# Two-layer diffusion trunk: the order of gathered rows and of latent attention's parts, and the engine that forms the table blocks' lower parts

## The chip, the cores and the metric

The kernel runs on one core of one Trainium2 chip. The metric is the device time of one execution in microseconds (us), the median of several. One execution of the kernel was also profiled; all rows below come from that one.

## The reference, cut to what matters

512 latent tokens (four tiles of 128) and 256 context tokens (two tiles), 1024 wide, go through two layers. Layer 0 mixes with neighbourhood attention and a gated delta net, layer 1 with multi-head latent attention (MLA). Each layer ends with a mixture of 16384 single-neuron experts ("PEER"). The last layer returns only the latent tokens.

```python
def layer(x, ctx):                       # cond gives shifts, scales and gates
    h, hc = modulate(rmsnorm(x)), modulate(rmsnorm(ctx))
    y, yc = even_mixer(h, hc) if layer == 0 else odd_mixer(h, hc)
    x   = x + g1 * y
    x   = x + g2 * peer_ffn(modulate(rmsnorm(x)))
    ctx = ...                            # the same, in layer 0 only

def odd_mixer(h, hc):
    p, pc = h @ w_in, hc @ w_in          # query, key/value and rotary parts
    q = mla_q(p); k, v = mla_kv(p); kc, vc = mla_kv(pc)
    return attention(q, concat(kc, k), concat(vc, v)) @ w_out

def peer_ffn(xb):                        # per token: 8 heads x 16 experts = 128
    expert, gate = route(xb)             # product keys, top 16
    act = gelu(xb . u_tab[expert])
    return sum_k gate_k * act_k * v_tab[expert_k]
```

## The kernel before

**PEER is computed in two ways.** The first three latent tiles (ND = 3) go densely through TensorE: for each of 128 table blocks of 128 experts the scores `sp` of all 384 tokens are computed, passed through gelu on ScalarE (`ge`), multiplied with the gates (`a`), and multiplied with the block of the v table into six accumulators (`acc`). Both tables are split into an upper and a lower part, since a product is made of three rounded ones: `uh` is ScalarE's rounding of the loaded block `ur`, and `ul = ur - uh`; `vh`, `vl` and `ah`, `al` likewise. 28 of the 128 blocks (FILL, the last in the loop) have their scores computed earlier, during other work; for them only `gel` (gelu'd scores) is loaded from memory, and no `u` block is needed. The two context tiles (names `cp`, layer 0 only) and the fourth latent tile (`xp` in layer 0, `yp` in layer 1, where the three dense tiles carry these names too) take the other way: for each of the 128 experts of a token GpSimd gathers one row of the u table and later one of the v table with an indirect DMA (128 tokens x 1024, 512 KB, L1227), and VectorE uses it (`jk` for u, L1245; `acc` for v, L1256). That makes 512 rows for the context and 256 for each fourth tile.

**Who sets the order of the rows.** The rows are made by generators in a queue. `pump(anchor, k)` takes k rows from the generator at the queue's head and places each on GpSimd behind the instruction `anchor`; six row buffers hold them, and a use stands four rows behind its gather. `tick(src, k)` does the same with a 128x1 copy on GpSimd that waits for `src`. In the dense loop a block pumps 3 rows in layer 0 and 2.5 in layer 1, a FILL block 2. `drain()` places all that are left. The context's rows start while layer 0 mixes the latent tokens and are still under way when the fourth tile's join the queue, behind them.

**The stages, by time in the profile.** Context mixing (0 to 450 us), latent mixing (to 1170), routes (to 1530), dense loop of layer 0 (to 2406), its FILL blocks (to 2567), MLA's projections (to 2759), MLA's attention (to 3010), routes (to 3360), dense loop of layer 1 (to about 4215), its FILL blocks (to 4341), end.

**MLA's projections** are made by three generators: `c` (context, two tiles), `x` (first three latent tiles), `t` (fourth tile). Each gives, in turn, the input projection `m_pi`, the normed and transposed `m_cT`, and the queries `m_qn` and `m_qr`. Their order in the program is written out by hand with calls of `nxt`. The part behind `drain()` needs what the last gathered rows add to: before the change that is the fourth latent tile. `norm1` loads a tile, scales its rows by the root mean square and transposes it on TensorE (`mc_hT`, `mx_hT`, `mt_hT` for the three).

**At the start**, the conditioning's first result `ar` (shifts and scales) goes to memory as a row, is loaded again as `ac_r`, and is transposed into columns `cols`, which ScalarE needs for each copy of a transposed tile out of PSUM (L235).

Of the kernel before, what the change touches and what calls it, by code (L numbers as in the profile page):

```python
# [9 lines left out]
F32 = mybir.dt.float32  # L10
# [9 lines left out]
P = 128  # L20
# [20 lines left out]
class Trunk:  # L41
    def __init__(self, tc, ins, out, dbg=None):
        self.tc = tc
        self.nc = tc.nc
        self.I = ins
        self.out = out
        self.dbg = dbg or {}
        self.flip = 0
        self.queue = []
        self.fill = iter(())  # L50
        self.aside = []
        self.rate = (3, 2.5)
        self.owed = 0
# [102 lines left out]
    def ada(self, pool, layer, groups, ps):  # L156


        nc = self.nc
        for g in groups:  # L160
            nm = f"{layer}{g}"
            acc = ps("ada_ps" + nm)
            for k in range(KD):
                w = pool.tile([P, 2048], F32, tag="aw", name=f"aw{nm}_{k}", bufs=3)
                nc.sync.dma_start(w, self.I["ada_w"][layer, k * P:(k + 1) * P, g * 2048:(g + 1) * 2048])
                yield
                for j in range(4):
                    self.mm(acc[32 * j:32 * j + 32, :], self.cond[:, k, :], w[:, j * 512:(j + 1) * 512],
                            start=(k == 0), stop=(k == KD - 1))
            b = pool.tile([P, 512], F32, tag="ab", name="ab" + nm)  # L170
            nc.sync.dma_start(b, self.I["ada_b"][layer, g])
            r = pool.tile([P, 512], F32, tag="ar", name="ar" + nm, bufs=2)
            nc.vector.tensor_add(r, acc, b)
            if g != 1:
                gn = pool.tile([P, 512], F32, tag="gn", name="gn" + nm)
                nc.sync.dma_start(gn, self.I["gain"][layer, g // 2])
                nc.vector.scalar_tensor_tensor(r, r, self.onep[:, g // 2:g // 2 + 1], gn,
                                               op0=ALU.add, op1=ALU.mult)
            nc.sync.dma_start(self.rowd[layer][g], r)

    def more(self, k):

# [5 lines left out]

    def ada_cols(self, layer):

        self.cols = self.rowpool.tile([P, 4, P], F32, tag="cols", name="cols")
        with self.tc.tile_pool(name=f"ac{layer}", bufs=1) as pool:
            r = pool.tile([P, 512], F32, name=f"ac_r{layer}")
            self.nc.sync.dma_start(r, self.rowd[layer][0])
            pt = self.ps("cols_ps")
            for b in range(4):
                self.tr(pt[:, b * P:(b + 1) * P], r[:, b * P:(b + 1) * P])
            self.nc.vector.tensor_copy(self.cols, pt)

    def mod_col(self, half, kb, s):  # L200
        r = 64 * half + 32 * (kb // 4) + s
# [586 lines left out]
    def odd_mixer(self, xs, cs, dst, open_xT, gathered):  # L788
# [4 lines left out]
        with ExitStack() as st:  # L793
            mc = st.enter_context(self.tc.tile_pool(name="mla_c", bufs=1, side="right"))
            hTc = mc.tile([P, KD, NC_], F32, name="m_hTc")
            self.norm1(cs, 1, hTc, "mc")
            self.wpool = st.enter_context(self.tc.tile_pool(name="mla_w", bufs=4, side="right"))
            yp = st.enter_context(self.tc.tile_pool(name="mla_y", bufs=1, side="right"))
            yT = yp.tile([P, 8, NX], F32, name="yT1")
# [4 lines left out]
            with ExitStack() as ist:  # L804
# [102 lines left out]

                c, x, t = part(1, hc, 2, 0, hTc), part(0, hx, ND, NC_, hTx), part(0, ht, 1, NC_ + ND * P, hTx)
                nxt = lambda g: next(g, None)
                nxt(c)  # L910
                self.norm1(xs[:ND], 0, hTx, "mx")
                nxt(c)
                nxt(x)
                nxt(c)
                nxt(x)
                nxt(c)
                nxt(x)
                nxt(x)
                nxt(x)
                self.drain()  # L920
                self.norm1(xs[ND:], 0, hTx[:, :, :P], "mt")
                nxt(x)
                nxt(t)
                nxt(t)
                nxt(x)
                nxt(x)
                for _ in t:
                    pass
            gathered()
            with self.tc.tile_pool(name="mla_at", bufs=2) as ap, self.tc.tile_pool(name="mla_a4", bufs=3) as a4:  # L930
# [264 lines left out]
    def peer_gather(self, xs, dst, routes, s, layer, nm):  # L1195


        self.queue.append(self.gather_slots(xs, dst, routes, s, layer, nm))

    def pump(self, anchor, k):  # L1200

# [13 lines left out]
    def gather_slots(self, xs, dst, routes, s, layer, nm):  # L1215
# [2 lines left out]
        gp = self.gpool  # L1218
        later = lambda: tc.high_priority(offset=-LATER)

        lag, wait = 4, []

        def row(tab, idx, j, name, use):

# [113 lines left out]
    def expert_scores(self, pool, b, xT, layer, nm, ps):  # L1338
# [5 lines left out]
        ul = pool.tile([P, KD, P], F32R, tag="ul", name=nm + f"_ul{b}")  # L1344
        uv = ur.rearrange("p (k e) -> p k e", e=P)
        nc.scalar.copy(uh, uv)  # L1346
        anchor = nc.gpsimd.tensor_sub(ul, uv, uh)  # L1347

        def go():
            sp = ps(nm + f"_sp{b}")  # L1350
# [9 lines left out]
    def peer_dense(self, xs, xT, up, layer, nm, done):  # L1360
# [3 lines left out]
        with ExitStack() as st:  # L1364
# [4 lines left out]
            def load(b):  # L1369
# [12 lines left out]
                vh = r3.tile([P, D], F32R, tag="vh", name=nm + f"_vh{b}", bufs=3)  # L1382
                vl = r3.tile([P, D], F32R, tag="vl", name=nm + f"_vl{b}", bufs=3)
                nc.scalar.copy(vh, vr)
                if b in FILL:
                    anchor = nc.gpsimd.tensor_sub(vl, vr, vh)  # L1386
                else:
                    nc.vector.tensor_sub(vl, vr, vh)
                self.pump(anchor, self.rate[layer] if b not in FILL else 2)
                return go, vh, vl  # L1390

            def gated(b, ge):
# [72 lines left out]
    def build(self):  # L1465
        nc, tc, I = self.nc, self.tc, self.I
        with ExitStack() as st:
# [13 lines left out]
            with ExitStack() as l0:  # L1481
# [24 lines left out]
                with ExitStack() as cst:  # L1506
                    with self.banks("cm", 5, 2, 1):
                        ast = ExitStack()
                        ap = ast.enter_context(tc.tile_pool(name="ada", bufs=1))
                        weave(self.ada(ap, 0, (0,), self.ps))  # L1510
                        self.ada_cols(0)
                        self.aside += [self.ada(ap, 0, (1, 2), self.side), self.ada(ap, 1, (0, 1, 2), self.side)]
                        xT = []
                        weave(self.even_mixer(src[0], c1, 1, "c", opener(cst, "cp_xT", NC_, ast.close), 0, xT))
# [142 lines left out]
```

## Time and profile before

| what | value |
|---|---|
| median of 3 timed runs | 4376.23 us (4374.13 to 4380.3) |
| profiled execution, own time | 4360.89 us |
| its span on the core | 4359.1 us |
| TensorE (PE) busy | 3943.7 us, 90% of the span |
| VectorE (DVE) busy | 3497.9 us, 80% |
| GpSimd (POOL) busy | 2035.1 us, 47% |
| ScalarE (ACT) busy | 1613.3 us, 37% |
| moved by DMA | 1113.89 MB, mean 256 GB/s |

PE is the matmul engine, PEld its weight loads, which overlap matmuls. DVE is VectorE, ACT ScalarE, POOL GpSimd, SP the engine whose queue issues most DMAs. "Idle before" a group is the time for which its engine stood still just ahead of its instructions, and behind the arrow stands what ended that. The share of 90% is a mean over stages with different limits. The profiled execution is 15.3 us shorter than the median, and what lies around its span is 1.8 us.

### The profile page before, as it was taken

How to read it: one execution, taken by the hardware profiler on the slowest of the kernel's cores; microseconds unless marked ns; L12 is line 12 of the kernel's file. 1: busy time of each engine (PE TensorE's matmuls, PEld its weight loads, DVE VectorE, ACT ScalarE, POOL GpSimd, SP SyncE). 2: the span in 40 equal slices, each digit the busy share in tenths (PEclk: the TensorE clock that was granted, in tenths of full speed). 3: DMA queues.
4: the chain of work that ended last, by engine and by line, in shares of the span. 5: the costliest groups of instructions: out<-in, count | busy, mean ns of one | idle time of the engine just before them, and what ended most of it. 6: DMA issues, size and time to landing. Idle time of an engine off the chain costs nothing.

```text
span 4359.1 us, 58568 instructions
## 1 busy us (share of the span) xinstructions
PE 3943.7 (90%) x20450; PEld 3198.6 (73%) x20450; DVE 3497.9 (80%) x6787; ACT 1613.3 (37%) x2929; POOL 2035.1 (47%) x1467
## 2 busy tenths in 40 slices
PE   7998888887799979999999865999999999999998
PEld 4676554685476767999999653775767899999986
DVE  1355989998899979999999977553998888888886
ACT  2353443353124523333333231562245333333333
POOL 0003367555630078767666856001200766666664
PEclk8999998998899989999999987999999999999999
DMA  8825498867934699999999978203246988888885
GB/s 305 295 105 158 166 323 315 279 222 242 316 118 159 227 365 353 346 344 352 337 345 332 325 260 301 67 26 103 73 161 232 346 317 308 309 305 312 309 287 178
DMA packets 484855, 1113.89 MB, mean 256 GB/s; under 512 B 38736, under 2 KB 256336, under 8 KB 475344
## 3 DMA queue, kind: packets, MB, share of 16 engines
q1 hardware_dynamic: 328896, 561.75, 37.4%
q0 software_dynamic: 147600, 537.40, 34.3%
q10 hardware_dynamic: 8064, 11.01, 0.7%
q8 instruction: 161, 2.64, 0.2%
q14 instruction: 134, 1.10, 0.1%
HBM read 1036.56 MB, written 73.92 MB: 255 GB/s over the span
## 4 chain that ended last, share of the span: by engine, by line
PE 61%; DVE 20%; DMA 8%; issue 6%; ACT 2%; POOL 2%; SPq 0%; DVEq 0%; ACTq 0%; POOLq 0%
PE yp_acc L75 10%; PE yp_sp L75 10%; PE xp_sp L75 9%; PE xp_acc L75 8%; PE mq_s L75 2%; DVE cp_acc L1256 2%; DMA cp_u<-peer_u,cp_idx 2%; PE x_p L75 1%; DVE cp_jk L1245 1%; PE yp_pg L75 1%; PE xp_pg L75 1%; DVE xp_acc L1256 1%; PE ada_ps L75 1%; PE yp_qy L75 1%; PE c_p L75 1%
## 5 line engine op out<-in xcount | busy, mean ns | idle before, releaser
L1227 POOL DMA_INDIRECT cp_u<-peer_u,cp_idx x256 | 318.0, 1242 | 316.0 <-DVE cp_jk L1245 222.6
L1347 POOL TENSOR_TENSOR yp_ul<-yp_ur,yp_uh 128x1024 fp32r<-128x1024 f32 x100 | 242.0, 2420 | 421.1 <-ACT yp_uh L1346 421.0
L75 PE MATMUL xp_sp<-xp_xT,xp_uh 128*128 128x384 f32 x1600 | 409.7, 337 | 12.4 <-ACT xp_uh L1346 12.4
L75 PE MATMUL yp_sp<-yp_xT,yp_uh 128*128 128x384 f32 x1600 | 408.8, 336 | 1.4 <-ACT yp_ge L1453 1.4
L1227 POOL DMA_INDIRECT cp_v<-peer_v,cp_idx x256 | 317.3, 1239 | 164.4 <-DVE cp_acc L1256 100.0
L75 PE MATMUL xp_acc<-xp_vh,xp_al 128*128 128x512 f32 x768 | 309.1, 402 | 31.9 <-DVE xp_al L1399 31.9
L1256 DVE SCALAR_TENSOR_TENSOR cp_acc<-cp_v,cp_act,cp_acc 128x1024 f32<-128x1024 f32 x254 | 330.9, 1303 | 6.9 <-DMA cp_v<-peer_v,cp_idx 4.4
L1394 DVE TENSOR_TENSOR yp_a<-yp_ge,yp_gb 128x384 f32<-128x384 f32 x100 | 237.3, 2373 | 123.3 <-ACT yp_ge L1356 123.3
L75 PE MATMUL xp_acc<-xp_vh,xp_ah 128*128 128x512 f32 x768 | 304.9, 397 | 15.8 <-ACT xp_ah L1398 15.8
L1347 POOL TENSOR_TENSOR xp_ul<-xp_ur,xp_uh 128x1024 fp32r<-128x1024 f32 x100 | 249.6, 2496 | 130.0 <-ACT xp_uh L1346 129.5
L75 PEld LDWEIGHTS xp_sp<-xp_xT,xp_uh 128*128 128x128 f32 x1600 | 293.2, 189 | 20.6 <-ACT xp_uh L1346 13.0
L75 PE MATMUL yp_acc<-yp_vh,yp_al 128*128 128x512 f32 x768 | 302.5, 394 | 5.5 <-DVE yp_al L1399 5.5
L75 PE MATMUL xp_acc<-xp_vl,xp_ah 128*128 128x512 f32 x768 | 304.8, 397 | 0.0
L75 PE MATMUL yp_acc<-yp_vl,yp_ah 128*128 128x512 f32 x768 | 301.6, 393 | 2.6 <-POOL yp_vl L1386 2.6
L75 PE MATMUL yp_acc<-yp_vh,yp_ah 128*128 128x512 f32 x768 | 299.9, 390 | 2.7 <-ACT yp_ah L1398 2.7
L75 PEld LDWEIGHTS yp_sp<-yp_xT,yp_uh 128*128 128x128 f32 x1600 | 292.4, 188 | 9.7 <-ACT yp_ge L1453 2.0
L75 PE MATMUL yp_sp<-yp_xT,yp_ul 128*128 128x384 f32 x800 | 269.4, 337 | 3.2 <-POOL yp_ul L1347 3.2
L75 PE MATMUL xp_sp<-xp_xT,xp_ul 128*128 128x384 f32 x800 | 269.8, 337 | 1.4 <-POOL xp_ul L1347 1.4
L1394 DVE TENSOR_TENSOR xp_a<-xp_ge,xp_gb 128x384 f32<-128x384 f32 x100 | 206.3, 2063 | 45.7 <-ACT xp_ge L1356 45.7
L1057 POOL TENSOR_TENSOR yp_wql<-yp_wq,yp_wqh 128x1024 fp32r<-128x1024 f32 x16 | 38.7, 2420 | 369.1 <-DMA yp_wq<-peer_w_q 311.5
L1346 ACT CAST yp_uh<-yp_ur 128x1024 fp32r<-128x1024 f32 x100 | 105.2, 1052 | 270.5 <-issue 214.7
L1398 ACT CAST xp_ah<-xp_a 128x384 fp32r<-128x384 f32 x128 | 65.8, 514 | 367.7 <-DVE xp_a L1394 323.5
(1479 smaller groups left out, 10753.1 us busy)
## 6 DMA issues: line engine op xcount, KB each, us to landing
xp_ur<-peer_uT SPq DMA_DIRECT2D x128, 512.0 KB, 5.7
xp_vr<-peer_v SPq DMA_DIRECT2D x128, 512.0 KB, 6.1
yp_ur<-peer_uT SPq DMA_DIRECT2D x128, 512.0 KB, 4.8
yp_vr<-peer_v SPq DMA_DIRECT2D x128, 512.0 KB, 4.9
aw<-ada_w SPq DMA_DIRECT2D x48, 1024.0 KB, 7.0
gdram<-xp_go SPq DMA_DIRECT2D x12, 2048.0 KB, 6.9
xp_gb<-gdram SPq DMA_DIRECT2D x32, 768.0 KB, 9.2
gdram<-yp_go SPq DMA_DIRECT2D x12, 2048.0 KB, 7.0
```

What stands on the lines that cost most here:

```text
L75: self.nc.tensor.matmul(out, lhsT, rhs, start=start, stop=stop)
L1057: self.pump(nc.gpsimd.tensor_sub(wl, raw, wh), 0)
L1227: d = nc.gpsimd.indirect_dma_start(out=r, out_offset=None, in_=tab, in_offset=bass.IndirectOffsetOnAxis(ap=idx[:, j:j + 1], axis=0))
L1245: return nc.vector.scalar_tensor_tensor(junk, u, 1.0, h2, op0=ALU.mult, op1=ALU.mult, accum_out=act[:, j:j + 1])
L1256: i = nc.vector.scalar_tensor_tensor(acc, v, act[:, j:j + 1], acc, op0=ALU.mult, op1=ALU.add)
L1346: nc.scalar.copy(uh, uv)
L1347: anchor = nc.gpsimd.tensor_sub(ul, uv, uh)
L1394: nc.vector.tensor_mul(a.rearrange("p (g t) -> p g t", t=32), ge.rearrange("p (g t) -> p g t", t=32), gbs[b // 4][:, :, b % 4, :])
L1398: nc.scalar.copy(ah, a)
```

## The change

It has four parts. (1) The first conditioning result is transposed straight from SBUF (`turn_cols`) without the way through memory. (2) A new generator of rows goes to the queue's head (`insert(0, ...)`), and the list of rows that wait for their use is shared between generators (`self.wait`), so the fourth tile's 256 rows are gathered ahead of what is left of the context's. (3) In the odd mixer the parts' order is `x`, `t`, then `drain()`, then `c`: the last rows are now the context's. (4) `ul` and FILL's `vl` are subtracted on VectorE and not on GpSimd, and the anchor of a block's rows is a `tick` on `vh`, which ScalarE makes.

```diff
@@ ada (layer 0, first group)
             nc.sync.dma_start(self.rowd[layer][g], r)
+            if not (layer or g):
+                self.turn_cols(r)
...
+    def turn_cols(self, r):
+        self.cols = self.rowpool.tile([P, 4, P], F32, tag="cols", name="cols")
+        pt = self.ps("cols_ps")
+        for b in range(4):
+            self.tr(pt[:, b * P:(b + 1) * P], r[:, b * P:(b + 1) * P])
+        self.nc.vector.tensor_copy(self.cols, pt)
@@ odd_mixer
-            self.norm1(cs, 1, hTc, "mc")
...
-                nxt(c)
                 self.norm1(xs[:ND], 0, hTx, "mx")
-                nxt(c)
                 nxt(x)
-                nxt(c)
-                nxt(x)
-                nxt(c)
-                nxt(x)
-                nxt(x)
-                nxt(x)
-                self.drain()
                 self.norm1(xs[ND:], 0, hTx[:, :, :P], "mt")
                 nxt(x)
                 nxt(t)
+                nxt(x)
                 nxt(t)
                 nxt(x)
                 nxt(x)
+                nxt(t)
+                nxt(x)
+                nxt(t)
+                self.drain()
+                self.norm1(cs, 1, hTc, "mc")
+                nxt(c)
+                for _ in x:
+                    pass
+                nxt(c)
                 for _ in t:
+                    pass
+                for _ in c:
                     pass
@@ peer_gather
-        self.queue.append(self.gather_slots(xs, dst, routes, s, layer, nm))
+        self.queue.insert(0, self.gather_slots(xs, dst, routes, s, layer, nm))
@@ gather_slots
-        lag, wait = 4, []
+        lag, wait = 4, self.wait
@@ expert_scores
-        anchor = nc.gpsimd.tensor_sub(ul, uv, uh)
+        anchor = nc.vector.tensor_sub(ul, uv, uh)
@@ peer_dense, load(b)
-                if b in FILL:
-                    anchor = nc.gpsimd.tensor_sub(vl, vr, vh)
-                else:
-                    nc.vector.tensor_sub(vl, vr, vh)
-                self.pump(anchor, self.rate[layer] if b not in FILL else 2)
+                nc.vector.tensor_sub(vl, vr, vh)
+                self.tick(vh, self.rate[layer] if b not in FILL else 2)
```

On GpSimd's queue late in layer 0's dense loop, before the change, each block has one subtraction and three gathered rows, by then of the fourth tile's v table:

```order
L1347 TENSOR_TENSOR xp_ul_19375<-xp_ur_19372,xp_uh_19374 128x1024
L1227 DMA xp_v_2_19384<-peer_v,xp_idx_10594 128x1024
L1227 DMA xp_v_3_19388<-peer_v,xp_idx_10594 128x1024
L1227 DMA xp_v_4_19392<-peer_v,xp_idx_10594 128x1024
L1347 TENSOR_TENSOR xp_ul_19451<-xp_ur_19448,xp_uh_19450 128x1024
```

With the change, at about the same place of GpSimd's queue:

```order
L1298 CAST tick<-xp_vh_19716 128x1
L1235 DMA cp_v_8_19722<-peer_v,cp_idx_3833 128x1024
L1235 DMA cp_v_9_19725<-peer_v,cp_idx_3833 128x1024
L1235 DMA cp_v_10_19728<-peer_v,cp_idx_3833 128x1024
L1298 CAST tick<-xp_vh_19790 128x1
```

The full-width subtraction is gone, a 128x1 copy stands in its place, and the rows are those of the context's second tile; as many rows as before are left for the stages that follow.

On VectorE's queue in the middle of the same loop, one block before the change:

```order
L1388 TENSOR_TENSOR xp_vl_14677<-xp_vr_14674,xp_vh_14676 128x1024
L1394 TENSOR_TENSOR xp_a_14644<-xp_ge_14642,xp_gb_14458 128x384
L1256 SCALAR_TENSOR_TENSOR cp_acc_13007<-cp_v_68_14614,cp_act_7245,cp_acc_13007 128x1024
L1399 TENSOR_TENSOR xp_al_14647<-xp_a_14644,xp_ah_14646 128x384
L1256 SCALAR_TENSOR_TENSOR cp_acc_13007<-cp_v_69_14680,cp_act_7245,cp_acc_13007 128x1024
L1256 SCALAR_TENSOR_TENSOR cp_acc_13007<-cp_v_70_14683,cp_act_7245,cp_acc_13007 128x1024
```

And with the change:

```order
L1399 TENSOR_TENSOR xp_a_14763<-xp_ge_14761,xp_gb_14562 128x384
L1355 TENSOR_TENSOR xp_ul_14867<-xp_ur_14864,xp_uh_14866 128x1024
L1404 TENSOR_TENSOR xp_al_14766<-xp_a_14763,xp_ah_14765 128x384
L1393 TENSOR_TENSOR xp_vl_14875<-xp_vr_14870,xp_vh_14874 128x1024
L1253 SCALAR_TENSOR_TENSOR xp_jk_92_14882,xp_act_12417<-xp_u_92_14732,x_o3h_9061 128x1024
L1253 SCALAR_TENSOR_TENSOR xp_jk_93_14886,xp_act_12417<-xp_u_93_14801,x_o3h_9061 128x1024
L1253 SCALAR_TENSOR_TENSOR xp_jk_94_14890,xp_act_12417<-xp_u_94_14805,x_o3h_9061 128x1024
```

`ul` of a later block now stands between `a` and `al`, where one row's use stood, and the three uses follow in one run.

On TensorE's queue in MLA's projections, before the change, behind the last work that does not need the drained rows:

```order
L75 MATMUL m_qn_21683<-cqT,m_wuq_21681 128x384 x3
L75 MATMUL m_qn_21705<-cqT,m_wuq_21681 128x384 x3
L78 MATMUL mt_hT_21730<-ident,mt_x_21713 128x128
...
L75 MATMUL m_qn_21762<-cqT,m_wuq_21755 128x384 x3
L75 MATMUL m_pi_0_21770<-m_wi_21768,m_hTx 128x256 x8
L75 MATMUL m_pi_0_21782<-m_wi_21780,m_hTx 128x128 x8
L75 MATMUL m_pi_0_21794<-m_wi_21792,m_hTx 128x256 x8
L75 MATMUL m_pi_0_21806<-m_wi_21804,m_hTx 128x64 x8
L75 MATMUL m_qn_21850<-cqT,m_wuq_21848 128x384 x3
```

With the change, from the first instruction that needs a drained row on:

```order
L79 MATMUL mc_hT_22103<-ident,mc_x_22053 128x128
L79 MATMUL mc_hT_22103<-ident,mc_x_22054 128x128
L76 MATMUL m_pi_0_22112<-m_wi_22110,m_hTc 128x256 x8
L76 MATMUL m_pi_1_22122<-m_wi_22110,m_hTc 128x256 x8
L76 MATMUL m_pi_0_22134<-m_wi_22132,m_hTc 128x64 x8
L76 MATMUL m_pi_1_22144<-m_wi_22132,m_hTc 128x64 x8
L76 MATMUL m_qn_22156<-cqT,m_wuq_22154 128x384 x3
...
L79 MATMUL m_krp<-ident,m_krt_22184 128x128
...
L76 MATMUL v_0_22265<-wuv0h,ckvTh 128x256
```

Behind the drained rows there stand now the context's 16 transposes and its projection, which has no query part, eight `m_qn` groups of three and five or six small transposes; the fourth tile's projection, its queries and its rotary products, which stood there before, have moved ahead of them.

## Rows read from the trace of the kernel before

**Rows 1.** The page's first part: busy time, share and instructions of each engine.

```profile
PE 3943.7 (90%) x20450; PEld 3198.6 (73%) x20450; DVE 3497.9 (80%) x6787; ACT 1613.3 (37%) x2929; POOL 2035.1 (47%) x1467
```

**Rows 2.** Windows: stretch, length, engines' busy time, granted clock, DMA share, GB/s.

```profile
core 0: us, PE busy (x) PEld busy (x) DVE busy (x) ACT busy (x) POOL busy (x), PEclk, DMA share, GB/s
1530.00:1690.00 160.00, 126.18 (x573) 106.07 (x573) 136.97 (x155) 42.89 (x59) 127.60 (x79) 0.92 0.99 361
1700.00:2400.00 700.00, 700.00 (x3541) 637.26 (x3540) 653.84 (x640) 244.72 (x338) 506.70 (x337) 1.00 0.94 342
2406.00:2567.00 161.00, 131.77 (x516) 102.57 (x515) 152.38 (x110) 42.07 (x55) 136.76 (x81) 0.93 0.94 323
...
2700.00:2720.00 20.00, 0.00 (x0) 0.00 (x0) 11.86 (x10) 0.00 (x0) 3.78 (x3) 0.50 0.69 252
```

**Rows 3.** Timeline of one dense block: start, duration, engine, instruction.

```profile
2005.75 0.49 ACT L1356 ACTIVATE xp_ge<-xp_sp 128x384 f32<-128x384 f32 x1
2005.93 2.40 POOL L1347 TENSOR_TENSOR xp_ul<-xp_ur,xp_uh 128x1024 fp32r<-128x1024 f32 x1 [0.35 <-ACT xp_uh L1346]
...
2005.95 3.46 DVE L1388 TENSOR_TENSOR xp_vl<-xp_vr,xp_vh 128x1024 fp32r<-128x1024 f32 x1
...
2008.85 0.51 PE L75 MATMUL xp_sp<-xp_xT,xp_uh 128*128 128x384 f32 x2
...
2009.34 0.55 DVE L1394 TENSOR_TENSOR xp_a<-xp_ge,xp_gb 128x384 f32<-128x384 f32 x1
...
2013.82 1.22 DVE L1388 TENSOR_TENSOR xp_vl<-xp_vr,xp_vh 128x1024 fp32r<-128x1024 f32 x1
```

**Rows 4.** Groups of instructions in 1700 to 2400 us, GpSimd's and VectorE's.

```profile
L1347 POOL TENSOR_TENSOR xp_ul<-xp_ur,xp_uh 128x1024 fp32r<-128x1024 f32 x84 | 208.3, 2480 | 121.7 <-ACT xp_uh L1346 121.4
...
L1394 DVE TENSOR_TENSOR xp_a<-xp_ge,xp_gb 128x384 f32<-128x384 f32 x85 | 187.0, 2200 | 41.3 <-ACT xp_ge L1356 41.3
L1245 DVE SCALAR_TENSOR_TENSOR xp_jk<-xp_u,x_o3h 128x1024 bf16<-128x1024 f32 x128 | 155.7, 1216 | 1.9 <-DMA xp_u<-peer_u,xp_idx 0.5
L1256 DVE SCALAR_TENSOR_TENSOR cp_acc<-cp_v,cp_act,cp_acc 128x1024 f32<-128x1024 f32 x108 | 139.1, 1288 | 2.0 <-DMA cp_v<-peer_v,cp_idx 0.8
```

**Rows 5.** Groups of TensorE in 1530 to 1690 us.

```profile
L75 PE MATMUL xp_acc<-xp_vh,xp_ah 128*128 128x512 f32 x74 | 30.8, 416 | 15.8 <-ACT xp_ah L1398 15.8
```

**Rows 6.** Groups of TensorE and ScalarE in 2406 to 2567 us.

```profile
L75 PE MATMUL xp_acc<-xp_vh,xp_al 128*128 128x512 f32 x172 | 73.4, 427 | 29.2 <-DVE xp_al L1399 29.2
...
L1384 ACT CAST xp_vh<-xp_vr 128x1024 fp32r<-128x1024 f32 x27 | 28.4, 1051 | 69.6 <-DMA xp_vr<-peer_v 66.2 <-POOL xp_vl L1386 3.4
```

**Rows 7.** GpSimd's waits in 2560 to 2720 us: total, times, longest.

```profile
POOL tick L1290 <- ACT m_psb L83: 42.2, 2, 37.9
```

**Rows 8.** The critical chain in 2590 to 2765 us: start, duration, what.

```profile
2592.61 5.55 DMA m_wi<-mla_w_in
2598.30 13.01 PE m_pi L75 x64
...
2710.49 1.29 DVE xp_acc L1256
...
2724.39 1.97 PE mt_hT L78 x8
...
2731.84 10.42 PE m_pi L75 x64
...
2758.98 4.56 PE v L75 x36
```

**Rows 9.** Timeline of the start.

```profile
40.52 2.19 ACT L230 ACTIVATE c_x<-c_x,c_r 128x1024 f32<-128x1024 f32 x2 [1.02 <-DVE c_r L128]
...
43.69 1.12 PE L78 MATMUL cols_ps<-ident,ac_r 128*128 128x128 f32 x4 [8.70 <-DMA ac_r<-row]
...
45.63 1.02 ACT L235 ACTIVATE c_hT<-c_hT,cols 128x256 f32<-128x256 f32 x2 [2.92 <-DVE cols L198]
```

**Rows 10.** Groups of TensorE in 4200 to 4360 us.

```profile
L75 PE MATMUL yp_acc<-yp_vh,yp_al 128*128 128x512 f32 x186 | 73.8, 397 | 4.8 <-DVE yp_al L1399 4.8
L75 PE MATMUL yp_acc<-yp_vl,yp_ah 128*128 128x512 f32 x186 | 73.4, 395 | 2.6 <-POOL yp_vl L1386 2.6
```

More of the change, by code (lines that the diff above doesn't have):

```diff
@@ L49, in __init__ @@
         self.queue = []
+        self.wait = []
         self.fill = iter(())
@@ L189, in ada_cols @@
     def ada_cols(self, layer):
-        self.cols = self.rowpool.tile([P, 4, P], F32, tag="cols", name="cols")
         with self.tc.tile_pool(name=f"ac{layer}", bufs=1) as pool:
@@ L194, in ada_cols @@
             self.nc.sync.dma_start(r, self.rowd[layer][0])
[L195 to L198, printed above, removed]
+            self.turn_cols(r)
+    def turn_cols(self, r):
[4 more added lines that the diff above has]
+        self.nc.vector.tensor_copy(self.cols, pt)
     def mod_col(self, half, kb, s):
@@ L1510, in build @@
                         weave(self.ada(ap, 0, (0,), self.ps))
-                        self.ada_cols(0)
                         self.aside += [self.ada(ap, 0, (1, 2), self.side), self.ada(ap, 1, (0, 1, 2), self.side)]
```

## The prediction

> **What bounds the kernel now.** I read the page's shares first, then windows of each stage, then for the stages where TensorE has gaps the groups with what ended their idle time, a timeline of one block, GpSimd's waits and the critical chain. TensorE is busy for 90% of the span [rows 1]; the windows say where the other tenth lies. In the dense loop's steady part it is busy for 700 of 700 us at full clock, so nothing that other engines gain there shows [rows 2]. Early in that loop it loses 160 - 126.2 = 33.8 us, and in FILL 161 - 131.8 = 29.2 us; in both the DMA share is 0.94 to 0.99 [rows 2]. In MLA's projections it is empty for a whole window of 20 us [rows 2]: the chain goes through the last gathered row (2710.49), then a store, a load and a norm, to the fourth tile's transposes at 2724.39 [rows 8].
>
> What bounds VectorE in the loop is partly not its own work. A `vl` subtraction took 3.46 us beside a GpSimd `ul` that had begun 0.02 us earlier and ran for 2.40; another took 1.22 with none beside it [rows 3]. Likewise `a` takes 2.20 us on average and 0.55 alone [rows 3, 4]. So a two-input VectorE operation stands still while GpSimd subtracts.
>
> **Steady dense blocks: 0.** 84 blocks in 700 us are 8.33 us each [rows 4]. With the change VectorE does, per block, `a` 0.55, `ul` and `vl` 1.22 each (`ul` has `vl`'s shape), `al` as long as `a` by its shape, 0.55, and three uses at 1.22 to 1.29, 3.7 to 3.9 [rows 3, 4]: 7.2 to 7.4 us, under 8.33. Now it is 653.84 / 84 = 7.8 [rows 2, 4]. GpSimd loses 2.48 us a block [rows 4]. TensorE's work is unchanged, and it covers all of this; without that cover the loop could fall by at most the 0.4 to 0.6 us a block that VectorE gains. What is tight is the order: `ul` stands behind `a`, `a` behind `ge`. `ge` ends at 2006.24 and the next scores begin at 2008.85 [rows 3]; `a` and `ul` take 1.77 of these 2.61 us, so 0.84 is spare. The `tick` waits for `vh`, behind which rows now stand in GpSimd's in-order queue; GpSimd already waits 121.4 us of the 700 for ScalarE's `uh` [rows 4], and it loses its subtractions, so rows should come no later.
>
> **Early dense blocks (1530 to 1690): -3.** Here more rows than the three per block run, and TensorE waits 15.8 us for `ah`, so for `a`'s engine [rows 5]. VectorE is busy 137.0 of 160 us, the DMA engines 0.99 at 361 GB/s [rows 2]. Bounds: 0, if the bytes set the pace; -15.8, if that wait goes. The share of 0.99 speaks for the first; -3.
>
> **FILL (2406 to 2567): -5.** TensorE waits 29.2 us for `al` [rows 6], and VectorE is busy 152.4 of 161 us, part of it in the shared lock. A block moves two rows, a v block, its share of gates and its scores, (2 x 512 + 512 + 192 + 192) KB, at 323 GB/s and a share of 0.94 [rows 2]. After the change VectorE does `a`, `al`, `vl` and two uses, 0.55 + 0.55 + 1.22 + 2.58 = 4.9 us [rows 3, 4] of the 161 / 28 = 5.75 that a block takes, so it stops being the bound and the transfers become it: ScalarE's `vh` waits 66.2 us for `vr` already [rows 6]. Bounds: 0, and -29.2 if TensorE never waited. If the share rose from 0.94 to that of the early blocks, 0.99, the stretch would be 161 x 0.94 / 0.99 = 153, or -8; I take -5, for the rows' latency at the loop's turn.
>
> How much a full DMA system gives is where a rule bears. The row: 361 GB/s at a share of 0.99 [rows 2]. The Trainium skill ("DMA: Bandwidth & Descriptors", section "Where 436 GB/s comes from") gives 436 GB/s as the ceiling on the SBUF side and about 358 as one core's share of the memory. By 436 FILL would be an estimated 161 x 323 / 436 = 119 us, under TensorE's own work, so it would win all 29 us; by 358 an estimated 145, -16. The trace agrees with the second ceiling and not with the first: no stretch shown here is above 361.
>
> **MLA's projections: -10.** First the drain. GpSimd stands for 37.9 us before MLA's first rows, at a tick on the input projection [rows 7]; that projection waited for weights, issued at 2592.61, and went to the context's part first, 13.0 us [rows 8]. With the change the weights' loads stand right behind the latent tiles' loads on SP's queue, and `x` is first, so rows should begin some microseconds earlier. Against that, five more query weights (393 KB each, 2 MB) must pass before the drain's end, 6 us at 342 GB/s [rows 2]. The number of rows in the drain is the same. Bounds: +6 and -13; -1.
>
> Then what follows the last row. Row, gate, residual, store, load and norm are as long as before (2710.49 to 2724.39, 13.9 us), only for the context's second tile. From there to `v` it was 34.6 us: transposes, the fourth tile's projection (10.4), then its queries, rotary products and `m_cT` [rows 8]. Now: 16 transposes for both tiles and their copies, 4 to 5; the context's projection, 10 to 13 (it was 13.0, at a low clock behind a pause, and it has 64 matmuls like the fourth tile's 10.4); eight `m_qn` groups of three, 24 matmuls at about the 0.4 or 0.3 us that their widths took, 7 to 8, which hide the norm of the result; transposes, 2. Sum 23 to 28, so -7 to -11; I take -9. The work of the fourth tile that moves ahead is not free, but it fills TensorE's hole of over 20 us before the last row [rows 2]: its projection, queries and rotary products are 34.6 - 2 (transposes) - 8 (the queries that stay behind) = 25 us at most, and in part they were waiting. What of it doesn't fit delays `mc_hT`: bound +5, inside the range.
>
> **FILL of layer 1: -4.** There are hardly any rows here. TensorE waits 4.8 us for `al` and 2.6 for GpSimd's `vl` [rows 10]. With `vl` at 1.22 and not 2.40 on the path from `vh`, and no lock, bounds are 0 and -7.4; the middle.
>
> **Start: -2.** The copies out of PSUM wait for `cols`, from `ac_r`, until 45.63 [rows 9]. With `cols` made from SBUF the scaled tile, ready at 42.71, ends last; with the one transposing step between (45.63 - 44.6, about 1 us) the copies begin at 43.7: -1.9. Bounds 0 (if weights end last) and -2.9.
>
> **Sum.** 0 - 3 - 5 - 10 - 4 - 2 = -24 us. The profiled execution took 4360.89 us, its span 4359.1; it would be 4337. The timed median is 4376.23, 15.3 us above it; I carry the difference over: **4352 us**. 0.2%, 8.75 us, is about what a measurement of this kernel can tell from no change.
>
> **Rivals.**
>
> *The rows no longer hold MLA up* (0.13). If GpSimd's pause of 37.9 us shrinks by half, the drain ends 19 us earlier instead of 1: -42 in all, 4334. For it: the window before the projection isn't full, since the loads are issued late [rows 8]. Against: GpSimd's ticks still wait for `m_psb`, made of the first projection, whose tile `mx` must come from the dense loop's end anyway.
>
> *Transfers hide it* (0.22). VectorE is relieved, but early blocks and FILL move the same bytes at shares of 0.99 and 0.94 [rows 2], and the drain pays its 2 MB more. Left: start -2, MLA's end -9, drain +3, layer 1's FILL -1: -9, 4367. That is the border of what can be told.
>
> *The change doesn't do what it says* (0.05). If the long `a` and `vl` come from something other than GpSimd's subtraction, such as the row gathers, VectorE's block is 2.20 + 1.50 + 1.22 + 0.55 + 3.8 = 9.3 us, over 8.33: the steady loop would grow by about 0.9 us on 85 blocks, +80, 4430. Against: the lone 0.55 and 1.22 in a stretch full of gathers [rows 3].
>
> *VectorE's order becomes the bound* (0.08). A row that lands late holds all behind it in VectorE's queue, now `ul` too, which GpSimd used to make by itself. If `a` begins later by more than the spare 0.84 us, each further tenth lengthens the block by a tenth. One use (1.29) in between costs 0.45 a block: 85 blocks of layer 0, +38 - 24 = +14, 4390; with layer 1's blocks more. For it: three uses now stand in one run, and the DMA share of 0.94 leaves little for a late row. Against: VectorE waits only 1.9 and 2.0 us of 700 for rows now [rows 4].
>
> **Chances and range.** The forecast has 0.52. It reaches 4340 to 4363. The range takes in the first rival and the hidden case with the bounds of MLA: 4326 to 4371. Faster by over 0.2% (under 4367.5): 0.52 + 0.13 + half of the hidden case, and the forecast's own tail taken off, 0.75; slower by over 0.2% (over 4385): 0.09; the same: 0.16.
>
> **What would show it.** In the profile after: `a` near 0.55 and `vl` and `ul` near 1.22 in the steady loop, TensorE still without gaps there, about 8.33 us a block; FILL of layer 0 near 156 us with a DMA share of 0.97; GpSimd's first MLA rows some microseconds earlier, and some 23 to 28 us from the transposes of the context's last tile to `v`; `cols` before the scaled context. The prediction is wrong if `sp` waits for `ul` in steady blocks, if TensorE's waits for `al` in FILL go entirely, if GpSimd waits long at ticks on `vh`, or if the last rows end much earlier or later than 2710 less the gains before.

## The result, and the profile after

The changed kernel takes 4317.94 us (median of 4 runs, 4313.45 to 4322.59) against 4375.18 us for the kernel before: a ratio of 0.987, 95% interval 0.9857 to 0.9882, about 57 us less. The forecast was 24 us less, and 4318 lies below its range. Its profiled execution has a span of 4317.7 us, 41.4 us less than before's. The missing 15 us are the kernel before's own: a second profile of it (below) has a span of 4374.0 us, so the first one was a quick execution, and I compare with both.

Stages are measured on TensorE, from the first and last starts of a tile's matmuls. Of the kernel before (its first profile) and then of the changed kernel the lines are, with first and last start at the end of each:

```profile
L75 PE MATMUL xp_sp<-xp_xT,xp_uh x1600: 333/334/689, 1550.8 to 2403.1; 128*128 128x384 f32 x178
L75 PE MATMUL xp_acc<-xp_vh,xp_ah x768: 387/389/628, 1563.8 to 2569.7; 128*128 128x512 f32 x192
L75 PE MATMUL v<-wuv0h,ckvTh x12: 276/281/358, 2759.0 to 2763.0; 128*128 128x256 f32 x12
...
L76 PE MATMUL xp_sp<-xp_xT,xp_uh x1600: 333/334/686, 1558.9 to 2394.1; 128*128 128x384 f32 x178
L76 PE MATMUL xp_acc<-xp_vh,xp_ah x768: 387/389/792, 1570.4 to 2533.9; 128*128 128x512 f32 x192
L76 PE MATMUL v<-wuv0h,ckvTh x12: 276/281/357, 2726.7 to 2730.7; 128*128 128x256 f32 x12
L76 PE MATMUL yp_sp<-yp_xT,yp_uh x1600: 332/338/688, 3345.7 to 4176.6; 128*128 128x384 f32 x178
L76 PE MATMUL yp_acc<-yp_vh,yp_ah x768: 389/389/497, 3361.5 to 4302.9; 128*128 128x512 f32 x192
```

"Loop" is from the first to the last score matmul, "FILL" from there to the last output matmul with `ah`, "MLA" from there to the first `v`. The same differences for every kernel of this study, in us:

| kernel | loop, layer 0 | FILL, layer 0 | MLA | loop, layer 1 | FILL, layer 1 |
|---|---|---|---|---|---|
| before | 852.3 | 166.6 | 189.3 | 831.7 | 134.4 |
| before, second profile | 852.3 | 173.4 | 191.2 | 833.0 | 134.8 |
| changed | 835.2 | 139.8 | 192.8 | 830.9 | 126.3 |
| e1, engines alone | 833.9 | 141.1 | 202.9 | 831.4 | 123.8 |
| e2, order alone | 852.0 | 168.2 | 178.4 | 832.4 | 135.8 |
| e4, FILL's `vl` alone | 852.1 | 139.7 | 204.6 | 832.7 | 124.2 |
| e5, a subtraction more in FILL | 836.5 | 166.7 | 189.0 | 830.7 | 126.6 |
| e9, a subtraction more in the loop | 880.3 | 149.9 | 197.7 | 830.2 | 126.0 |
| e6, 3.25 rows per block | 839.8 | 139.8 | 159.4 | 830.6 | 126.9 |
| e6b, 3.5 rows per block | 859.1 | 143.5 | 133.5 | 828.5 | 127.3 |
| e7, 3 rows per FILL block | 835.4 | 140.5 | 181.7 | 829.8 | 125.6 |
| e8, both 3.25 and 3 | 836.8 | 143.6 | 150.2 | 830.7 | 126.6 |

Against the second profile of before (4374.0), the changed one's 56.3 us less are: loop -17.1, FILL of layer 0 -33.6, FILL of layer 1 -8.5, layer 1's loop and what lies ahead of it -3.6, MLA +1.6, and +4.8 ahead of the loop. That last one is no effect of the change to be made out: the loop begins between 1544.0 and 1558.9 us in the eight profiles of kernels with the new start, which hardly differ up to there.

Windows of the changed kernel, to set beside [rows 2]; the first two are the loop's beginning, then FILL and the two ahead of MLA's last row:

```profile
core 0: us, PE busy (x) PEld busy (x) DVE busy (x) ACT busy (x) POOL busy (x), PEclk, DMA share, GB/s
1558.00:1658.00 100.00, 94.28 (x454) 84.49 (x455) 85.42 (x126) 33.74 (x45) 62.23 (x52) 0.95 1.03 387
1658.00:1758.00 100.00, 98.64 (x492) 87.90 (x491) 92.67 (x140) 35.18 (x49) 70.86 (x56) 1.00 1.02 384
...
2394.00:2534.00 140.00, 128.05 (x542) 101.46 (x541) 118.84 (x136) 41.44 (x57) 96.42 (x77) 0.99 0.98 352
...
2660.00:2680.00 20.00, 0.00 (x0) 0.00 (x0) 16.68 (x14) 0.00 (x0) 15.99 (x12) 0.50 0.99 368
2680.00:2700.00 20.00, 0.00 (x0) 0.00 (x0) 8.48 (x12) 1.35 (x3) 0.00 (x0) 0.50 0.47 163
```

FILL moves more per microsecond than before (352 against 323 GB/s), at a share of 0.98. All of FILL in the kernel before:

```profile
2403.10:2569.70 166.60, 137.37 (x540) 107.24 (x540) 156.51 (x118) 43.08 (x57) 138.92 (x83) 0.93 0.93 320
```

By these two windows it moved 53.3 MB before (166.6 us at 320 GB/s) and 49.3 now (140 at 352). At 352 GB/s the bytes of before would take some 151 us, an estimate: about 15 us of the 27 go with the higher rate, and about 12 with the bytes that are no longer moved here. Its groups on TensorE, to set beside [rows 6], and on VectorE:

```profile
L76 PE MATMUL xp_acc<-xp_vh,xp_al 128*128 128x512 f32 x179 | 71.9, 402 | 9.8 <-DVE xp_al L1404 9.6
...
L1264 DVE SCALAR_TENSOR_TENSOR cp_acc<-cp_v,cp_act,cp_acc 128x1024 f32<-128x1024 f32 x49 | 62.7, 1279 | 0.3
L1393 DVE TENSOR_TENSOR xp_vl<-xp_vr,xp_vh 128x1024 fp32r<-128x1024 f32 x27 | 33.0, 1223 | 15.9 <-ACT xp_vh L1392 14.6 <-issue 1.0
L1404 DVE TENSOR_TENSOR xp_al<-xp_a,xp_ah 128x384 fp32r<-128x384 f32 x29 | 16.0, 551 | 0.1
L1399 DVE TENSOR_TENSOR xp_a<-xp_gel,xp_gb 128x384 f32<-128x384 f32 x28 | 15.5, 552 | 3.0 <-DMA xp_gel<-gedram 2.9
```

TensorE's wait for `al` fell from 29.2 to 9.8 us, which is 19 of the 27; new waits of 2.2 us for `ah` and `vl` stand against it. The rest is TensorE's own time: for nearly as many matmuls (540 and 542) it was busy for 137.4 us at a mean granted clock of 0.93 and is now busy for 128.1 at 0.99, so more of the stretch ran at the upper of its two levels (1.2 and 2.4 GHz). What raised the clock was not tried apart from the shorter waits. The second profile of the kernel before shows the same groups of VectorE in its FILL (2406.4 to 2579.8 us):

```profile
L1256 DVE SCALAR_TENSOR_TENSOR xp_acc<-xp_v,xp_act,xp_acc 128x1024 f32<-128x1024 f32 x54 | 81.7, 1512 | 3.8 <-DMA xp_v<-peer_v,xp_idx 2.8
L1399 DVE TENSOR_TENSOR xp_al<-xp_a,xp_ah 128x384 fp32r<-128x384 f32 x29 | 44.3, 1527 | 0.1
L1394 DVE TENSOR_TENSOR xp_a<-xp_gel,xp_gb 128x384 f32<-128x384 f32 x28 | 29.6, 1058 | 11.5 <-DMA xp_gel<-gedram 10.7
```

`al` took 1.53 us, now 0.55; `a` 1.06, now 0.55; a use 1.51, now 1.28. The 54 uses are now 49 in this stretch: the number matters below. In the loop (1700 to 2390 us of the changed kernel; beside [rows 4]) both subtractions take 1.22 and `a` 0.55, as forecast, and VectorE waits 82.8 us for `vh` there, so it has room:

```profile
L1393 DVE TENSOR_TENSOR xp_vl<-xp_vr,xp_vh 128x1024 fp32r<-128x1024 f32 x83 | 101.7, 1226 | 82.8 <-ACT xp_vh L1392 82.8
L1355 DVE TENSOR_TENSOR xp_ul<-xp_ur,xp_uh 128x1024 fp32r<-128x1024 f32 x83 | 101.1, 1219 | 0.4 <-ACT xp_uh L1354 0.4
L1399 DVE TENSOR_TENSOR xp_a<-xp_ge,xp_gb 128x384 f32<-128x384 f32 x84 | 46.4, 553 | 0.2 <-ACT xp_ge L1364 0.2
```

The critical chain through MLA, beside [rows 8], and GpSimd's longest wait there, beside [rows 7]:

```profile
2568.47 31.38 PE m_pi L76 x192
...
2687.54 1.30 DVE cp_acc L1264
2688.86 1.24 DVE cp_acc L1267
...
2701.33 3.76 PE mc_hT L79 x16
2705.09 10.43 PE m_pi L76 x64
2715.52 7.94 PE m_qn L76 x48
...
2726.69 4.56 PE v L76 x36
```

```profile
POOL tick L1298 <- ACT m_psb L84: 27.5, 3, 24.7
```

From the transposes to `v` it is 25.4 us and not 34.6: that is the forecast's 23 to 28, and -9.2 for its -9. But the last row is used 153.6 us after FILL's last matmul (2533.9 to 2687.5), and it was 140.8 before (2569.7 to 2710.5): the drain is 13 us longer, and 10 longer than in the second profile of before (143.5).

### The profile page after: what moved, and what is told of

The parts are those of the page before. It is cut to its first block, busy times and chain, and to the rows that moved or that the text cites. A ratio compares the mean times of both kernels' runs of the same rounds, so it can differ in the third digit from the quotient of the medians.

```text
span 4317.7 us, 58680 instructions
## 1 busy us (share of the span) xinstructions
PE 3934.8 (91%) x20450; PEld 3204.0 (74%) x20450; DVE 3328.4 (77%) x7043; ACT 1626.5 (38%) x2929; POOL 1712.8 (40%) x1443
## 4 chain that ended last, share of the span: by engine, by line
PE 64%; DVE 19%; DMA 10%; issue 4%; ACT 3%; POOL 1%; SPq 0%; DVEq 0%; ACTq 0%; POOLq 0%
PE yp_acc L76 11%; PE yp_sp L76 11%; PE xp_sp L76 9%; PE xp_acc L76 9%; DVE cp_acc L1264 2%; PE mq_s L76 2%; PE x_p L76 1%; DMA xp_ur<-peer_uT 1%; PE yp_pg L76 1%; PE xp_pg L76 1%; DMA cp_u<-peer_u,cp_idx 1%; DMA xp_vr<-peer_v 1%; PE yp_qy L76 1%; PE c_p L76 1%; PE ada_ps L76 1%
## 5 line engine op out<-in xcount | busy, mean ns | idle before, releaser
L1235 POOL DMA_INDIRECT cp_u<-peer_u,cp_idx x256 | 308.4, 1205 | 326.2 <-DVE cp_jk L1253 222.9
L1298 POOL COPY tick<-yp_vh 128x1 f32<-128x1 f32 x104 | 119.5, 1149 | 520.7 <-ACT yp_vh L1392 520.7
L1393 DVE TENSOR_TENSOR yp_vl<-yp_vr,yp_vh 128x1024 fp32r<-128x1024 f32 x128 | 156.7, 1224 | 155.7 <-ACT yp_vh L1392 155.6
L1393 DVE TENSOR_TENSOR xp_vl<-xp_vr,xp_vh 128x1024 fp32r<-128x1024 f32 x128 | 156.7, 1225 | 102.6 <-ACT xp_vh L1392 101.2
L1298 POOL COPY tick<-xp_vh 128x1 f32<-128x1 f32 x128 | 136.9, 1069 | 243.1 <-ACT xp_vh L1392 242.7
L1354 ACT CAST xp_uh<-xp_ur 128x1024 fp32r<-128x1024 f32 x100 | 105.3, 1053 | 273.0 <-PE xp_sp L76 217.5
L1392 ACT CAST xp_vh<-xp_vr 128x1024 fp32r<-128x1024 f32 x128 | 134.5, 1051 | 176.4 <-PE xp_acc L76 99.3
```

The lines of the kernel that those rows point to most:

```text
L1235: d = nc.gpsimd.indirect_dma_start(out=r, out_offset=None, in_=tab, in_offset=bass.IndirectOffsetOnAxis(ap=idx[:, j:j + 1], axis=0))
L1298: self.pump(self.nc.gpsimd.tensor_copy(t, src[:, 0:1]), k)
```

## The experiments

Two theories of the large term, FILL of layer 0. **A:** GpSimd's subtraction held VectorE, and the transfers had room for more. **B:** FILL was bound by transfers, as I had assumed, and shrank because the new order of rows took bytes out of it. A third reading is that the v block's buffer, which GpSimd no longer holds, made the difference.

**The kernel before, a second time.** No edit.

> The kernel before, once more, for a second profile of it. The timed median should be 4375 us within 0.2%. The changed kernel's profile is 8 us later than before's already at 1550 us, where the change has only moved the start, and before's profiled execution was 15 us shorter than its median. If that profile was a lucky one, this one shows the loop of layer 0 begin near 1559 us instead of 1551 and a span near 4373; if the change itself lengthened the mixing stage by 8 us, this one begins the loop near 1551 again.

Measured: 4371.69 us, ratio 1.0004 (0.9994 to 1.0013), and a span of 4374.0 us. The loop begins at 1554.1, between the two guesses, and FILL takes 173.4 us, 7 more than in the first profile. So 7 of the 15 us between the two profiles lie in FILL, and a few us at 1550 tell nothing.

**Engines alone (part 4).**

```diff
 # in the kernel before
-        anchor = nc.gpsimd.tensor_sub(ul, uv, uh)
+        anchor = nc.vector.tensor_sub(ul, uv, uh)
...
-                if b in FILL:
-                    anchor = nc.gpsimd.tensor_sub(vl, vr, vh)
-                else:
-                    nc.vector.tensor_sub(vl, vr, vh)
-                self.pump(anchor, self.rate[layer] if b not in FILL else 2)
+                nc.vector.tensor_sub(vl, vr, vh)
+                self.tick(vh, self.rate[layer] if b not in FILL else 2)
```

> Part 4 alone: both subtractions on VectorE and the ticks on the upper part, with the old order of rows and of MLA's parts. Theory A (GpSimd's subtraction held VectorE, the transfers had room): FILL of layer 0 shrinks from 167 us (last score matmul to last output matmul) to about 140, early blocks by about 15, FILL of layer 1 by 8, and some 10 of it is given back in MLA's drain: 30 to 45 us faster than before. Theory B (FILL shrank since the order of rows moved other bytes into it): FILL stays at 160 or more, and the kernel is less than 15 us faster.

Measured: 4326.55 us, ratio 0.9899 (0.9882 to 0.9915), 44 us faster. Loop -18, FILL of layer 0 141.1 us, FILL of layer 1 -11, MLA 12 to 14 us longer. As A had it.

**Order alone (all but part 4).** The same lines turned back in the changed kernel.

> The whole change without part 4: GpSimd still forms the lower parts. Theory A: FILL of layer 0 stays near 165 us, MLA's stretch behind the last row is 9 us shorter, the start 2: 8 to 15 us faster than before. Theory B: FILL shrinks to about 140 here: 30 us faster or more.

Measured: 4361.03 us, ratio 0.9981 (0.9971 to 0.999), 8 us faster by the ratio, 10 by the medians. FILL of layer 0 stays at 168.2 us, so the rows' order doesn't shorten it: B falls. MLA is 178.4 us, 11 to 13 shorter than in both profiles of before.

**FILL's lower v part alone.**

```diff
 # in the kernel before; ul stays on GpSimd
-                if b in FILL:
-                    anchor = nc.gpsimd.tensor_sub(vl, vr, vh)
-                else:
-                    nc.vector.tensor_sub(vl, vr, vh)
-                self.pump(anchor, self.rate[layer] if b not in FILL else 2)
+                nc.vector.tensor_sub(vl, vr, vh)
+                if b in FILL:
+                    self.tick(vh, 2)
+                else:
+                    self.pump(anchor, self.rate[layer])
```

> The kernel before with only FILL's lower v part moved to VectorE and FILL's rows placed behind a tick on the upper part; the 100 other blocks as before. Theory A: FILL of layer 0 at about 140 us and FILL of layer 1 8 us shorter, early blocks unchanged, 10 given back in the drain: 20 to 28 us faster. Theory B: FILL of layer 0 at 160 or more, under 10 us faster.

Measured: 4344.6 us, ratio 0.9947 (0.9931 to 0.9964), 23 us faster by the ratio, 26 by the medians. FILL of layer 0 139.7, of layer 1 124.2, the loop unchanged at 852.1, MLA 204.6. These 28 + 28 subtractions alone bring all of both FILLs' gain, and the loop's 17 us belong to the other 100, `ul`.

**The subtraction back, with nothing that hangs on it.**

```diff
 # in the changed kernel
                 self.tick(vh, self.rate[layer] if b not in FILL else 2)
+                if b in FILL and not layer:
+                    lk = r3.tile([P, KD, P], F32, tag="lk", name=nm + f"_lk{b}", bufs=1)
+                    it = self.iota.unsqueeze(1).to_broadcast([P, KD, P])
+                    self.after(nc.gpsimd.tensor_sub(lk, it, it), self.anchor)
```

> The changed kernel with one more GpSimd subtraction of 128x1024 in each FILL block of layer 0, behind the block's tick; it reads a constant and nothing reads its result, so it frees and holds no buffer of the block. If the engines' shared port was what held FILL (theory A), VectorE's a, al and uses beside it get longer again (means of 1.0 us and more for a and al in FILL, 0.55 now) and FILL of layer 0 goes from 140 us back to 155 or more, less given back in the drain: 5 to 20 us slower than the changed kernel. If instead the hold on the v block's buffer or the later rows held it, FILL stays within 4 us of 140.

Measured: 4342.36 us, ratio 0.9928 (0.9906 to 0.9949), some 25 us slower than the changed kernel by the ratios, a little more than expected. FILL of layer 0 is 166.7 us again. Its groups on TensorE and VectorE:

```profile
L76 PE MATMUL xp_acc<-xp_vh,xp_al 128*128 128x512 f32 x179 | 74.5, 416 | 32.2 <-DVE xp_al L1408 32.2
...
L1264 DVE SCALAR_TENSOR_TENSOR cp_acc<-cp_v,cp_act,cp_acc 128x1024 f32<-128x1024 f32 x49 | 80.4, 1640 | 0.3
L1403 DVE TENSOR_TENSOR xp_a<-xp_gel,xp_gb 128x384 f32<-128x384 f32 x28 | 38.3, 1366 | 2.2 <-DMA xp_gel<-gedram 2.1
L1393 DVE TENSOR_TENSOR xp_vl<-xp_vr,xp_vh 128x1024 fp32r<-128x1024 f32 x27 | 38.0, 1407 | 0.9 <-ACT xp_vh L1392 0.9
```

And its window of FILL:

```profile
2392.00:2558.70 166.70, 134.51 (x542) 102.77 (x541) 163.27 (x135) 42.93 (x57) 142.12 (x105) 0.97 0.88 296
```

A subtraction that reads a constant and whose result nobody reads takes all 27 us away again. VectorE is busy for 163 of 167 us, uses take 1.64 and not 1.28, `a` 1.37 and not 0.55, and the DMA share drops to 0.88. No buffer explains that, and no later row either, since VectorE stood still for only 0.3 us ahead of its uses; A is shown. Which operations pay differs: here `a` most, then the uses and `vl`, while `al` stays at 0.55; before the change `al` most, then `a` and the uses. TensorE's waits are as long as before here (32.2 us) at a mean clock of 0.97, so the clock doesn't follow them alone.

**The same in the loop.** `if b in FILL` becomes `if b not in FILL` in that edit.

> The changed kernel with one more GpSimd subtraction of 128x1024 of a constant, whose result nobody reads, in each of the 100 blocks of layer 0 that are not FILL. If the shared port lengthened the loop's early blocks, the time from the first to the last score matmul goes from 835 us back to 850 or more, VectorE's a or uses get longer on average in the loop, and FILL stays near 140: 10 to 20 us slower than the changed kernel. If it was the order of the rows or the buffer of ul, the loop stays at 835.

Measured: 4358.74 us, ratio 0.9981 (0.9969 to 0.9992), almost all the gain gone, 48 us slower than the changed kernel where 10 to 20 had been expected. The loop takes 880.3 us. FILL, which was to stay near 140, took 149.9; why is open. Uses in 1700 to 2390 us:

```profile
L1264 DVE SCALAR_TENSOR_TENSOR xp_acc<-xp_v,xp_act,xp_acc 128x1024 f32<-128x1024 f32 x127 | 216.9, 1708 | 14.6 <-DMA xp_v<-peer_v,xp_idx 13.1
L1253 DVE SCALAR_TENSOR_TENSOR xp_jk<-xp_u,x_o3h 128x1024 bf16<-128x1024 f32 x85 | 147.0, 1730 | 6.0 <-DMA xp_u<-peer_u,xp_idx 5.0
```

The likely reason of the miss, read from VectorE's busy time: this kernel has VectorE do `ul` as well, 1.22 us a block more than before, and the lock on top, so that VectorE becomes the bound of the whole loop (busy 804 of 832 us in 1558 to 2390) and not of its beginning alone. So moving `ul` to VectorE pays only because it ends the lock; one such subtraction per block left on GpSimd would have made the change's loop slower than before's.

**More rows in the loop.** Where MLA's end waits for the last row, rows that are gathered earlier should help.

```diff
-        self.rate = (3, 2.5)
+        self.rate = (3.25, 2.5)
```

> The changed kernel with 3.25 rows per block and not 3 in layer 0's loop, 25 rows fewer for MLA's drain. In the drain TensorE stands for about 48 us of waiting for the last row. If those rows are what it waits for and the steady loop has room for a quarter of a row more per block (VectorE 7.4 of 8.33 us, some 353 GB/s against the 374 to 405 seen), the time from the last FILL matmul to v falls from 193 to about 155 to 165 us: 25 to 40 us faster than the changed kernel. If the loop has no room, its 835 us grow by 15 or more and eat it up: within 10 us of the changed kernel.

Measured: 4286.22 us, ratio 0.9805 (0.9784 to 0.9825), 28 us faster than the changed kernel by the ratios. MLA 159.4 us, the loop 839.8, 4.6 more. With `(3.5, 2.5)`:

> The same with 3.5 rows per block, 50 rows fewer for the drain, almost all of them. With room in the loop: TensorE's wait in MLA gone but for the norm chain, 40 to 50 us faster than the changed kernel. Without room (VectorE 8.05 of 8.33 us, 369 GB/s): the loop grows by 20 us or more and the total is no better than with 3.25.

Measured: 4289.67 us, ratio 0.9808 (0.9787 to 0.9829). MLA falls to 133.5 us, but the loop grows to 859.1, and FILL by 4. Its windows of the loop:

```profile
1558.00:1900.00 342.00, 329.99 (x1617) 294.31 (x1618) 306.73 (x454) 114.46 (x158) 233.25 (x189) 0.98 1.02 382
1900.00:2418.00 518.00, 510.35 (x2551) 457.26 (x2550) 463.36 (x485) 173.64 (x243) 342.31 (x276) 1.00 0.99 363
```

VectorE has some time left (770 of 860 us busy), but it now stands and waits for rows. The changed kernel (1558 to 2394 us) first, then this one (1558 to 2418):

```profile
L1264 DVE SCALAR_TENSOR_TENSOR xp_acc<-xp_v,xp_act,xp_acc 128x1024 f32<-128x1024 f32 x127 | 162.9, 1283 | 6.5 <-DMA xp_v<-peer_v,xp_idx 3.5
...
L1264 DVE SCALAR_TENSOR_TENSOR xp_acc<-xp_v,xp_act,xp_acc 128x1024 f32<-128x1024 f32 x127 | 163.0, 1283 | 34.6 <-DMA xp_v<-peer_v,xp_idx 32.7
L1253 DVE SCALAR_TENSOR_TENSOR xp_jk<-xp_u,x_o3h 128x1024 bf16<-128x1024 f32 x128 | 156.4, 1222 | 21.5 <-DMA xp_u<-peer_u,xp_idx 19.5
```

So at 3.5 rows land too late for VectorE, the loop grows, and the total is no better than at 3.25. Whether full transfers or late issues make them late was not tried: the share of 0.99 alone doesn't tell, since the changed kernel's early blocks moved 387 GB/s and these 518 us moved 363.

**More rows in FILL.** `2)` becomes `3)` in `self.tick(vh, ... else 2)`.

> The changed kernel with 3 rows and not 2 per FILL block of layer 0 (and of layer 1, which has hardly any left): 28 rows fewer for the drain, but in a stretch whose DMA share is 0.98 already. If FILL is bound by transfers now, it grows by about what the drain shrinks (28 rows of 512 KB at 352 GB/s are 42 us): within 10 us of the changed kernel. If it still had room, 25 us faster or more.

Measured: 4305.49 us, ratio 0.9849 (0.983 to 0.9868), some 9 us faster than the changed kernel by the ratios, close to the first guess, but not for its reason. FILL doesn't grow (140.5), since the rows' uses fall behind anyway (50 in the stretch, 49 with 2 rows per block); MLA is 11 us shorter. The rows stand in GpSimd's queue ahead of the pause and not behind it: the pause is 11.6 us, 24.7 in the changed kernel.

**Both.** `(3.25, 2.5)` and 3 rows per FILL block.

> The changed kernel with both 3.25 rows per block and 3 per FILL block in layer 0. With 3.25 alone TensorE works in MLA almost up to the last row, and what is left is the store, load and norm of the context's tile and query weights that land late. If the row of 3 in FILL helps by filling GpSimd's pause behind FILL, the last row ends before TensorE's other work does, and some 5 to 10 us more are won than with 3.25 alone; if TensorE's own work now sets the end, both are the same within 5 us.

Measured: 4277.8 us, ratio 0.9789 (0.9763 to 0.9814), the quickest version here, about 92 us less than the kernel before and 35 less than the changed one by the ratios. Its interval overlaps that of 3.25 alone, so the 8 us between their medians are not settled; MLA at 150.2 against 159.4 us speaks for them, FILL at 143.6 against 139.8 against them.

## Why the prediction was wrong

**Steady blocks, 0: right.** VectorE's operations took what was forecast, and TensorE had no gaps. Layer 1's loop stayed within 3 us.

**FILL of layer 0, -5: the step that failed.** It measured -27 and -34 against the two profiles. The prediction saw the lock, saw 152 of 161 us of VectorE and a wait of 29.2 us for `al`, and then let the transfers become the bound, since their share was 0.94. Two things were wrong in that. A share of 0.94 at 323 GB/s was read as nearly full, when early blocks of the same profile had moved 361 [rows 2]; the stretch had room for 352. And the floor of 153 us kept FILL's bytes fixed, while fewer rows came to be used in it (54 before, 49 now). The upper bound, -29.2, was in the prediction, and the value lay at it, though not by the wait alone: 9.8 us of that wait are left, and the shorter busy time of TensorE, which the prediction held fixed, made up for them. The rule weighed there fared no better: the Trainium skill ("DMA: Bandwidth & Descriptors", section "Where 436 GB/s comes from") has about 358 GB/s as one core's share, and I wrote that the trace agreed; the changed kernel moved 387 and 384 GB/s over 100 us each, above it and below the page's 436. Nor did the trace of before agree, since shorter windows of it lie above 361:

```profile
1590.00:1620.00 30.00, 23.80 (x104) 19.45 (x104) 27.08 (x37) 8.50 (x12) 24.95 (x16) 0.94 1.02 384
...
3400.00:3420.00 20.00, 19.11 (x95) 16.79 (x95) 16.85 (x23) 5.71 (x8) 17.28 (x11) 1.00 1.04 396
```

**The lock: right, and understated.** The Trainium skill ("SBUF — State Buffer", section "SBUF: two separate sides") states that VectorE and GpSimd share a port pair as an exclusive lock, held for a whole instruction, also by a VectorE operation with two SBUF inputs against a GpSimd operation that reads SBUF. The trace agrees: with the constant's subtraction beside them, `a` took 1.37 us and not 0.55, uses 1.64 and not 1.28. The rival that something other than GpSimd's subtraction lengthened them is out by the same run.

**Early blocks, -3: mis-sized.** The loop lost 17 us, all of it with part 4 (852.0 without, 833.9 with it alone). The prediction's own bound was -15.8. TensorE's wait for `ah`, 15.8 us in before's first 160 [rows 5], fell to 4.9 in the changed kernel (1538 to 1698 us):

```profile
L76 PE MATMUL xp_acc<-xp_vh,xp_ah 128*128 128x512 f32 x87 | 35.0, 403 | 4.9 <-ACT xp_ah L1403 4.9
```

Here too the DMA share of 0.99 was read as a wall, at 361 GB/s, and the changed kernel went through it at 387.

**MLA, -10: right for what was looked at, and one cost was not seen.** Order alone gave 11 to 13 us less: against the first profile 9.4 from the transposes on (34.6 to 25.2) and 1.4 in the drain (140.8 to 139.4), as worked out. But in every kernel in which `vl` has left GpSimd and rows hang on the tick, MLA is longer: 202.9 and 204.6 with the old order against 189.3 and 191.2, 189.0 and 192.8 with the new one against 178.4. "The number of rows in the drain is the same" holds for GpSimd's queue only. In VectorE's written order, 54 uses stand among FILL's last 28 `al` and 56 behind them before the change and with order alone; with `vl` moved it is 45 and 65. Nine uses went over into the drain, for which GpSimd had issued some 52 rows from 2605.5 to 2702.9 us before, 1.9 us each; 9 x 1.9 = 17 us estimated from that, 11 to 14 measured. FILL's win was partly given back there. That the uses went with the move is shown by the four kernels that have it; what made the scheduler place them so was not tried apart. It is their order and not FILL's length: with the constant's subtraction FILL is as long as before (166.7 us), the uses still stand 45 and 65, and MLA still takes 189.0.

**FILL of layer 1, -4: about double, -8.5** (its bound was -7.4), again the subtraction, by the fourth experiment.

**Start, -2: right.** The copies out of PSUM begin at 43.81 us, 43.7 by the forecast and 45.63 before [rows 9], and `c_v` begins between 51.8 and 53.7 us in the eight profiles with the new start and between 54.6 and 55.4 in the four with the old one. No run timed it by itself, and it is under what a timing can tell, so that any of it reaches the total is not shown.

**The rivals.** None of the four came true. GpSimd's pause did shrink, from 37.9 to 24.7 us, but its first tick came 39.8 us after FILL's last matmul and not 35.1. Transfers did not hide FILL's gain, the long operations came from the subtraction, and steady blocks kept TensorE without gaps. No rival had both stages lose their whole waits: early blocks at -15.8 and FILL at -29.2, with the rest as forecast, make -61 us or 4315, outside a range that was narrower than the bounds of its own terms. That 4318 lies near that sum is partly luck, since MLA brought nothing instead of -10.

**The sum** erred on one side, by taking the value near 0 in each stage with a high DMA share. The carried difference of 15 us between profile and median was no property of the kernel: the second profile of before stood at 4374.0, the changed kernel's at 4317.7, both near their medians.

## What to carry to other kernels

A GpSimd subtraction beside VectorE's work cost VectorE time here, 3.46 - 1.22 = 2.24 us for one instruction that met one of 2.40 [rows 3], and it did so even when it read a constant and nothing waited for it; look for means well above the shortest instance of the same shape, and try the work on VectorE if it fits there without the lock. Don't read a high DMA share as a bound before comparing its GB/s with the fastest stretch of the same profile. When a stage gets shorter, count what work stood among its instructions in each engine's order, the uses as well as the issues: what has moved behind the stage is paid in the next one.

## What was not expected of the hardware

The transfers reached 384 to 387 GB/s over 100 us at a share of 1.02 to 1.03, where 160 us of the kernel before had 361 at 0.99 [rows 2]: a share near 1 did not tell how much more a stretch could move. With a constant's subtraction in each block (e9) the first of these stretches, 1558 to 1658 us, fell back to 360 at 0.98. A GpSimd subtraction of a constant, with no reader, cost 166.7 - 139.8 = 26.9 us over 28 blocks, 0.96 us each, though nothing waits for it.
